# A two-layer diffusion backbone on one core: the order of seven products, the place of bank copies, and where the modulation is computed

## The chip, the cores and the metric

The kernel runs on one core of one Trainium2 chip. The metric is device time in microseconds (us). Before the change three runs gave 2406.03, 2399.41 and 2404.97 us, median 2404.97. PE is TensorE, PEld its weight loads, DVE is VectorE, ACT is ScalarE, POOL is GpSimd, SP is SyncE; a q behind a name (SPq, POOLq) is that engine's DMA queue.

## The reference, cut to what matters

Two streams of 256 tokens each, a latent one and a context one, go through two layers with the same weights. A layer is a half-step SwiGLU feed-forward, a token mixing (mLSTM and latent attention side by side), and a second half-step feed-forward. Each is preceded by a norm and modulated by nine rows that come from a conditioning vector:

```
mx = split(silu(c)     @ w_ada[l] + b_ada[l], 9)      # latent
mc = split(silu(c_ctx) @ w_ada[l] + b_ada[l], 9)      # context
x   = x   + 0.5*mx[2]*swiglu(rmsnorm(x,  g1)*(1+mx[1])+mx[0], w_ff1_up, w_ff1_dn)
ctx = ctx + 0.5*mc[2]*swiglu(rmsnorm(ctx,g1)*(1+mc[1])+mc[0], w_ff1_up, w_ff1_dn)
y_ctx, y_lat = token_mix(...)      # modulated by groups 3, 4; scaled by group 5
x   = x + mx[5]*y_lat
x   = x + 0.5*mx[8]*swiglu(rmsnorm(x, g3)*(1+mx[7])+mx[6], w_ff2_up, w_ff2_dn)
# the context stream does the same, but not behind the mixing of the last layer
```

The model width is 1024, the feed-forward width 2816. All is float32; the kernel computes each product as three matmuls of a high and a low part (hi*hi, lo*hi, hi*lo).

## The kernel before, in words

**Parts of a weight.** A weight block of 128x1024 is loaded into a buffer `st` (six of them), ACT copies it to a rounded high part `wh`, and DVE subtracts to get the low part `wl` (four buffers of each). This is `unit` for plain blocks and `Step.weights` with `parts7` for the blocks of the seven products.

**The seven products.** The second feed-forward of layer 0 and the first of layer 1 (`ff7`) go over both streams. Their up-projection treats the two halves of the width and the two streams as a 2x2 block product and uses seven products in place of eight. Four of the 22 blocks of the feed-forward width go the plain way (`FIRST`); the others are nine `Step`s of two blocks. A step needs four quarters of weights, a11, a12, a21, a22, and seven weights made from them: 1 is a11, 2 is a12, 4 is a22, 5 is a21+a22, 6 is 5+a11, 7 is a11+a21, 3 is 6+a12. Before the change DVE forms 5 (L715), and the other three sums are made by DMAs that POOL issues and that add into the buffer (`more`, L704). Each product is 24 matmuls. The results gather in three PSUM banks: 1, 6, 7 and 4 add up in A (rA), 2 and 3 in B (rB), 5 in C (rC). After 1, 6 and 7 ACT copies what bank A holds to a tile sa, sb or sc (L763) before the next of them adds to it. So product 6 cannot start until the copy behind 1 is done, 7 not until the copy behind 6, 4 not until the copy behind 7. The order of the products is a list in `ff7`, and each product's first matmul is held behind the last of the one before.

**Order on the engines.** The program is planned: an instruction has the place of its call, moved forward by `high_priority(offset)` (110 for the weights of a step, 150 for plain blocks, 40 for the bank copies), and a planner with a model of the times fixes one order for each engine, which each engine then works through in that order. `issue_after(x)` holds an instruction behind x on the same engine.

**Chunks.** The steps are done in chunks of one, four and four (`CHUNKS`). At the end of a chunk `last_blocks` multiplies what it gave by the down weights, eight blocks, and adds to the residual.

**Modulation.** Group g of layer l is computed by DVE: 8 blocks of 128 rows of w_ada, each loaded as two 128x512 pieces, and for each piece and stream one instruction that multiplies by the conditioning row and sums (L397). The class `Ada` holds a list of blocks; `drip` in the feed-forwards, and `Feed.pump` in the mixing, work it off as the stage goes on, and loads run two blocks ahead. On its first call it also loads and activates the conditioning rows (`silu_rows`: cb is the load, ACT and DVE make cs). Layer 0's second feed-forward computes groups 0 to 2 of layer 1; layer 1's first computes groups 3 to 6; the mLSTM part of layer 1's mixing computes groups 7 and 8. From group 5 on layer 1 needs the latent stream alone.

Of the kernel before, what the change touches and what calls it, by code (L numbers as in the profile page):

```python
# [50 lines left out]
SLOW = (3, 2)  # L51
EARLY = 2
SOON = 40
EVERY = 10
TAIL = 2
START = ((4, 4), (4, 4))
MARKS = (7, 7, 7, 7, 7, 7)
# [88 lines left out]
def body(ctx, tc, A):  # L146
# [183 lines left out]
        for s in range(2):  # L330
            mods[l, s] = cp.tile([P, 72], F32, name=f"mod{l}{s}")

    def silu_rows():

        res = {}
        for s in range(2):
            for q in range(2):
                v = act(F32, "cb")[:, :512]
                load(v, cc.partition_broadcast(P)[:, s, q * 512 : (q + 1) * 512])
                res[s, q] = act(F32, "cs")[:, :512]  # L340
                silu2(res[s, q], v)
        return res
# [39 lines left out]
    def ada_load(l, g, j):  # L382
# [4 lines left out]
            sts.append(st)  # L387
        return sts

    def ada_block(cb, l, g, j, sts):  # L390
        t = g * 8 + j
        streams = (0, 1) if l < DEPTH - 1 or g < 5 else (1,)
        for q, st in enumerate(sts):
            for s in streams:
                o = st if s == streams[-1] else act(F32, "junk")[:, :512]
                dst = mhalf[:, s, t : t + 1] if q else mods[l, s][:, t : t + 1]
                V.scalar_tensor_tensor(o, st, 0.5, cb[s, q], ALU.mult, ALU.mult, accum_out=dst)  # L397

    def ada_group_end(l, g):
        streams = (0, 1) if l < DEPTH - 1 or g < 5 else (1,)  # L400
        c = COLS["b_ada", l] + g * 8
        for s in streams:
            m = mods[l, s][:, g * 8 : g * 8 + 8]
            V.tensor_tensor(m, m, mhalf[:, s, g * 8 : g * 8 + 8], ALU.add)
            V.tensor_tensor(m, m, vecs[:, c : c + 8], ALU.add)
            if g % 3 == 1:
                gn = COLS[("g_n1", "g_n2", "g_n3")[g // 3], l]
                V.scalar_tensor_tensor(m, m, 1.0, vecs[:, gn : gn + 8], ALU.add, ALU.mult)
            elif g in (2, 8):
                V.tensor_scalar(m, m, 0.5, None, ALU.mult)  # L410

    class Ada:
# [8 lines left out]
            while len(self.loaded) < min(upto, self.n):  # L421
                self.loaded.append(ada_load(*self.todo[len(self.loaded)]))

        def next(self):
            if self.done < self.n:
                self.run((self.done + 1) / self.n)

        def run(self, frac):

            if self.cb is None:  # L430
                self.cb = silu_rows()
            while self.done < min(self.n, round(frac * self.n)):
                self.load(self.done + self.ahead)
                l, g, j = self.todo[self.done]
                ada_block(self.cb, l, g, j, self.loaded[self.done])
                if j == 7:
                    ada_group_end(l, g)
                self.done += 1
            self.load(self.done + self.ahead)
# [144 lines left out]
    def ff(l, f, streams, queue, after):  # L584
        g0 = 0 if f == 0 else 6
        cols = slice(0, T) if len(streams) == 2 else LAT
        n = T if len(streams) == 2 else HALF
        step = [0.0]

        def drip(w):  # L590
            step[0] += w
            if queue:
                queue.run(step[0] / (2 * CH + 0.7 * (2 * KB - 3)))

        def at(dst, part):
            return [d[:, part.start - cols.start : part.stop - cols.start] for d in dst]

        for c in range(2):
            blocks = range(c * CH, (c + 1) * CH)
            keys = {i: [("up", l, f, i, u) for u in range(2)] for i in blocks}  # L600
            gs = [pair(n) for _ in blocks]
            early = []
            if c == 0:
                for i in blocks[:2]:
                    early.append((i, units(keys[i], UW, 4)))
                    if ahead[0] > 1:
                        ahead[0] = EARLY
                for part in (LAT, CTX) if len(streams) == 2 else (LAT,):
                    for i, lhs in early:
                        up(part, hpairs(part), None, lhs, at(gs[i], part))  # L610
                drip(2.0)
            for i in blocks[len(early) :]:
                up(cols, hpairs(cols), keys[i], None, at(gs[i - c * CH], cols))
                drip(1.0)
                ahead[0] = AHEAD

            def make(nb, c=c):
                r = []
                for u, (a, b) in enumerate(DN_SPLIT):
                    r += units([("dn", l, f, c, nb, u)], (b - a) * P, b - a)  # L620
                drip(0.7)
                return r

            norms = {s: Norm((CTX, LAT)[s]) for s in streams} if c else None
            last_blocks(make, gs, streams, l, g0 + 2, norms, lambda s: after(norms[s], s))
        if queue:
            queue.run(1.0)

    hx = {}

    def shifted(nm, l, s, g):

# [51 lines left out]
    class Step:  # L686
# [18 lines left out]
            return self.st[n]  # L705

        def weights(self, r):
            with tc.high_priority(offset=AHEAD_S):
                if r == 1:
                    st = self.fresh("a", "a11")  # L710
                elif r == 2:
                    st = self.fresh("b", "a12")
                elif r == 5:
                    st = self.fresh("c", "a21")
                    V.tensor_tensor(st, st, self.fresh("d", "a22"), ALU.add)  # L715
                elif r == 6:
                    st = self.more("c", "a11")
                elif r == 7:
                    st = self.more("a", "a21")
                elif r == 3:  # L720
                    st = self.more("c", "a12")
                else:
                    st = self.st["d"]
                hi = wp.tile([P, UW], F32R, tag="wh", name="wh", bufs=WB)
                lo = wp.tile([P, UW], F32R, tag="wl", name="wl", bufs=WB)
                parts7(st, hi, lo)
            w = "p (b k n) -> p b k n"
            return hi.rearrange(w, b=2, k=4), lo.rearrange(w, b=2, k=4)

# [28 lines left out]
        def after(self, r):  # L758
            v, ps = self.v, self.ps
            if r in (1, 6, 7):  # L760
                with tc.high_priority(offset=SOON):
                    v[r] = self.tile("s" + "abc"[(1, 6, 7).index(r)])
                    S.activation(v[r], ps[1], AF.Copy)  # L763
            if r == 2:
                v[2] = self.tile("a7")
                with tc.high_priority(offset=SOON):
# [17 lines left out]
    def ff7(l, f, queue, after):  # L784
# [10 lines left out]
        for c, (first, n) in enumerate(CHUNKS):  # L795
            gs = []
            if first:
                keys = [[("up", l, f, i, u) for u in range(2)] for i in range(first)]
                early = [(i, units(keys[i], UW, 4)) for i in range(2)]
                for s, part in ((1, LAT), (0, CTX)):  # L800
                    for i, lhs in early:
                        if s:
                            gs.append({})
                        hi, lo = pair(HALF)
                        up(part, hpairs(part), None, lhs, (hi, lo))
                        gs[i][s] = hi, lo
                        if s == 0 and i == 1:
                            rest = differences()
                            next(rest)
# [6 lines left out]
            t0 += n  # L816
            for st in mine:
                t = st.t
                order = [(t, 1), (t, 2), (t, 6), (t + 1, 5), (t, 7), (t, 3), (t, 4)]
                if t == 0:  # L820
                    order.insert(0, (t, 5))
                if t == STEPS - 2:
                    order.insert(6, (t + 1, 1))
                if t == STEPS - 1:
                    order = [(t, 6), (t, 2), (t, 7), (t, 3), (t, 4)]
                for u, r in order:
                    mark = steps[u].product(r, mark)
                    drip(1 / 7)
                gs += [{s: st.dst[s][i] for s in (0, 1)} for i in range(2)]
# [9 lines left out]
            queue.run(1.0)  # L839


    def mix(l, queue, after):
        last = l == DEPTH - 1
        allc = slice(0, T)
        qc = LAT if last else allc
# [9 lines left out]
        class Feed:  # L855
# [3 lines left out]

            def __init__(self):  # L860
                self.items, self.chains, self.slow, self.done = [], [], [], set()
                self.pumps, self.queue = 0, None

            def add(self, key, gen):
                self.items.append((key, gen))
# [14 lines left out]
            def pump(self, n=1):  # L880
                self.draw(self.chains, n)
                for _ in range(n):
                    self.pumps += 1
                    if self.queue and self.pumps % EVERY == 0:
                        self.queue.next()
                    if self.pumps % SLOW[last] == 0:
                        self.draw(self.slow, 1)

# [660 lines left out]
        due = 0.0  # L1549
        for h, rate in chain(((-1, FEED[last][0]) for _ in mla()), ((h, FEED[last][1]) for h in mlstm())):  # L1550
            due += rate
            feed.queue = queue if h >= 0 else None
            feed.step(int(due), room_for(h))
            due -= int(due)

        if queue:
            queue.run(1.0)


        ys = []  # L1560
# [54 lines left out]

    for l in range(DEPTH):
        last = l == DEPTH - 1
        half(l, 0, Ada(0, range(2, 9), 2) if l == 0 else Ada(l, range(3, 7), 2), normed(l, None, 3))
        mix(l, Ada(l, range(7, 9), 2) if last else None, normed(l, 1, 6))
        half(l, 1, None if last else Ada(l + 1, range(3), 2), final if last else normed(l + 1, 0, 0))  # L1620

# [119 lines left out]
```

## Time and profile before

| | |
|---|---|
| median of 3 runs | 2404.97 us (2399.41 to 2406.03) |
| profiled execution, and its span | 2411.98 us, 2410.3 us |
| PE busy, DVE busy, ACT busy | 2313.2, 1746.2, 1093.2 us |
| granted TensorE clock, mean over the span | 0.982 |
| first seven-product stage (layer 0, second feed-forward) | 1026 to 1404 us |
| second seven-product stage (layer 1, first feed-forward) | 1404 to 1787 us |
| mixing of layer 1 | 1787 to 2207 us |
| last feed-forward (latent stream alone) | 2207 to the end |

How to read it: a wait is listed as who waited, for whom, the total, how often, and the longest. A row of the timeline has the start, the duration, engine, line, operation and tiles, and in brackets the idle time of that engine just before and what ended it. A clock of 1.00 is 2.4 GHz, 0.50 is 1.2 GHz.

### The profile page before, as it was taken

How to read it: one execution, taken by the hardware profiler on the slowest of the kernel's cores; microseconds unless marked ns; L12 is line 12 of the kernel's file. 1: busy time of each engine (PE TensorE's matmuls, PEld its weight loads, DVE VectorE, ACT ScalarE, POOL GpSimd, SP SyncE). 2: the span in 40 equal slices, each digit the busy share in tenths (PEclk: the TensorE clock that was granted, in tenths of full speed). 3: DMA queues.
4: the chain of work that ended last, by engine and by line, in shares of the span. 5: the costliest groups of instructions: out<-in, count | busy, mean ns of one | idle time of the engine just before them, and what ended most of it. 6: DMA issues, size and time to landing. Idle time of an engine off the chain costs nothing. (4 is left out here: it accounts for less than half of the span.)

```text
span 2410.3 us, 39446 instructions
## 1 busy us (share of the span) xinstructions
PE 2313.2 (96%) x15390; PEld 2101.8 (87%) x15390; DVE 1746.2 (72%) x3559; ACT 1093.2 (45%) x1778; POOL 147.2 (6%) x298
## 2 busy tenths in 40 slices
PE   7999999999999999999999999999899998999998
PEld 4888888888898888889999988999898797999998
DVE  6887787796577654487877678896768778876665
ACT  6322223567544442363534353443446564455443
POOL 1121110000100000000001000000000000000000
PEclk9999999999999999999999999999999999999999
DMA  9657545222222223446868526786722345455563
GB/s 331 196 158 229 158 143 164 77 63 62 68 76 76 71 79 96 124 104 186 216 175 195 148 79 201 186 245 166 200 80 82 89 130 168 140 168 156 171 207 105
DMA packets 117113, 347.66 MB, mean 144 GB/s; under 512 B 13886, under 2 KB 16190, under 8 KB 116926
## 3 DMA queue, kind: packets, MB, share of 16 engines
q1 hardware_dynamic: 100190, 287.47, 38.1%
q0 software_dynamic: 16736, 57.68, 10.8%
q8 instruction: 120, 1.97, 0.3%
q14 instruction: 67, 0.55, 0.1%
HBM read 341.95 MB, written 3.15 MB: 143 GB/s over the span
## 5 line engine op out<-in xcount | busy, mean ns | idle before, releaser
L246 ACT ACTIVATE wh<-st 128x1024 fp32r<-128x1024 f32 (+3 forms) x396 | 391.6, 992 | 674.2 <-issue 219.2
L248 DVE TENSOR_TENSOR wl<-st,wh 128x1024 fp32r<-128x1024 f32 (+3 forms) x396 | 450.0, 1140 | 221.5 <-ACT wh L246 220.0
L653 ACT ACTIVATE wh<-st 128x1024 fp32r<-128x1024 f32 x126 | 133.4, 1060 | 216.1 <-PE dn L511 63.1
L654 DVE TENSOR_TENSOR wl<-st,wh 128x1024 fp32r<-128x1024 f32 x126 | 153.6, 1221 | 39.4 <-ACT wh L653 39.2
L397 DVE SCALAR_TENSOR_TENSOR ada<-ada,cs 128x512 f32<-128x512 f32 x256 | 168.9, 688 | 17.1 <-DMA ada<-ada 17.0
L293 PE MATMUL p<-hl,wh 128*128 128x256 f32 (+1 forms) x536 | 180.1, 336 | 0.0
L292 PE MATMUL p<-hh,wh 128*128 128x512 f32 (+1 forms) x512 | 174.1, 340 | 0.0
L294 PE MATMUL p<-hh,wl 128*128 128x512 f32 (+1 forms) x512 | 173.3, 339 | 0.0
L505 DVE SCALAR_TENSOR_TENSOR x<-dn,mod,x 128x256 f32<-128x256 f32 x168 | 75.4, 479 | 98.7 <-PE dn L268 50.4
L397 DVE SCALAR_TENSOR_TENSOR junk<-ada,cs 128x512 f32<-128x512 f32 x192 | 124.4, 687 | 3.5 <-DMA ada<-ada 3.5
L741 PE MATMUL rA<-dh,wh 128*128 128x256 f32 x288 | 88.1, 306 | 37.0 <-ACT sa L763 35.6
L293 PE MATMUL pb<-hl,wh 128*128 128x512 f32 (+1 forms) x352 | 120.5, 342 | 0.0
L294 PE MATMUL pa<-hh,wl 128*128 128x512 f32 (+1 forms) x352 | 120.5, 342 | 0.0
L294 PE MATMUL pb<-hh,wl 128*128 128x512 f32 (+1 forms) x352 | 120.5, 342 | 0.0
L292 PE MATMUL pb<-hh,wh 128*128 128x512 f32 (+1 forms) x352 | 120.5, 342 | 0.0
L293 PE MATMUL pa<-hl,wh 128*128 128x512 f32 (+1 forms) x352 | 120.5, 342 | 0.0
L292 PE MATMUL pa<-hh,wh 128*128 128x512 f32 (+1 forms) x352 | 120.5, 342 | 0.0
L293 PEld LDWEIGHTS p<-hl,wh 128*128 128x128 f32 x536 | 101.4, 189 | 11.0
L294 PEld LDWEIGHTS p<-hh,wl 128*128 128x128 f32 x512 | 96.8, 189 | 11.3
L292 PEld LDWEIGHTS p<-hh,wh 128*128 128x128 f32 x512 | 96.9, 189 | 10.9
L268 PE MATMUL dn<-hi,wh 128*128 128x512 f32 (+1 forms) x278 | 101.1, 365 | 0.0
L268 PE MATMUL dn<-hi,wl 128*128 128x512 f32 (+1 forms) x278 | 101.1, 364 | 0.0
(438 smaller groups left out, 7190.4 us busy)
## 6 DMA issues: line engine op xcount, KB each, us to landing
st<-wall SPq DMA_DIRECT2D x372, 512.0 KB, 3.7
ada<-ada SPq DMA_DIRECT2D x176, 256.0 KB, 5.3
ada<-ada POOLq DMA_DIRECT2D x112, 256.0 KB, 3.5
st<-wall POOLq DMA_DIRECT2D x54, 512.0 KB, 5.7
st<-wall SPq DMA_DIRECT2D x56, 384.0 KB, 3.3
st<-wall SPq DMA_DIRECT2D x32, 320.0 KB, 3.0
cb<-cc SPq DMA_DIRECT2D x16, 256.0 KB, 4.4
x<-xT SPq DMA_DIRECT2D x8, 256.0 KB, 5.9
```

The source lines that it names most:

```text
L246: S.activation(hi[:, :n], st[:, :n], AF.Copy)
L248: V.tensor_tensor(lo[:, :n], st[:, :n], hi[:, :n].bitcast(F32), ALU.subtract)
L268: TE.matmul(ps, lhs[k][a][:, lsl], rhs[k][b][:, rsl], start=i == 0, stop=i == 3 * n - 1)
L292: TE.matmul(ps, a, b, start=first, stop=False)
L293: TE.matmul(ps, a, bl, start=False, stop=False)
L294: TE.matmul(ps, al, b, start=False, stop=final_)
L397: V.scalar_tensor_tensor(o, st, 0.5, cb[s, q], ALU.mult, ALU.mult, accum_out=dst)
L505: V.scalar_tensor_tensor(xs[nb][:, cols], ps[:, pcols], mod(l, s, g, nb), xs[nb][:, cols], ALU.mult, ALU.add)
L653: S.activation(hi, t, AF.Copy)
L654: V.tensor_tensor(lo, t, hi.bitcast(F32), ALU.subtract)
L741: mm = TE.matmul(ps[:, p * HALF : (p + 1) * HALF], w[x][:, p, k], hx["op", r][k][y], start=new and i == 0, stop=i + 1 == len(todo), skip_g ...
```

## The change

The list of products is reordered, so that 1 and 2 of the next step come in among the last of the present one. Bank copies are remembered in `snaps`, and the copy that makes a high part is held behind one of them (`BEFORE` says which). Weight 5 is now made by a load and an adding DMA, weight 3 by DVE from the buffers of 2 and 6. The conditioning rows are begun earlier in `ff7` (`begin`), for only the streams that are used. Group 7 moves to layer 1's first feed-forward, group 8 to its second, and the mixing computes none.

```
-EVERY = 10
+BEFORE = {5: 1, 7: 1, 3: 1, 1: 6, 4: 6, 2: 7, 6: 7}
...
-                queue.run(step[0] / (2 * CH + 0.7 * (2 * KB - 3)))
+                queue.run(min(1.0, step[0] / (CH - 1 if queue.n == KB else 2 * CH + 0.7 * (2 * KB - 3))))
...
-    hx = {}
+    hx, snaps = {}, {}
...
+        def begin(self):
+            l, g, _ = self.todo[0]
+            self.cb = silu_rows(streams_of(l, g))
...
                 elif r == 5:
-                    st = self.fresh("c", "a21")
-                    V.tensor_tensor(st, st, self.fresh("d", "a22"), ALU.add)
+                    self.fresh("c", "a21")
+                    st = self.more("c", "a22")
...
                 elif r == 3:
-                    st = self.more("c", "a12")
+                    st = self.st["b"]
+                    V.tensor_tensor(st, st, self.st["c"], ALU.add)
                 else:
-                    st = self.st["d"]
+                    st = self.fresh("d", "a22")
...
-                parts7(st, hi, lo)
+                snap = snaps.get(BEFORE[r])
+                with tc.issue_after(snap) if snap else nullcontext():
+                    S.activation(hi, st, AF.Copy)
+                V.tensor_tensor(lo, st, hi.bitcast(F32), ALU.subtract)
...
-                    S.activation(v[r], ps[1], AF.Copy)
+                    snaps[r] = S.activation(v[r], ps[1], AF.Copy).ins
...
                         gs[i][s] = hi, lo
+                        if s and i and queue:
+                            queue.begin()
...
-                order = [(t, 1), (t, 2), (t, 6), (t + 1, 5), (t, 7), (t, 3), (t, 4)]
+                order = [(t, 6), (t + 1, 5), (t, 7), (t, 3), (t + 1, 1), (t, 4), (t + 1, 2)]
                 if t == 0:
-                    order.insert(0, (t, 5))
-                if t == STEPS - 2:
-                    order.insert(6, (t + 1, 1))
+                    order = [(0, 5), (0, 1), (0, 2)] + order
                 if t == STEPS - 1:
                     order = [(t, 6), (t, 2), (t, 7), (t, 3), (t, 4)]
+                elif t == STEPS - 2:
+                    order.pop()
...
-        half(l, 0, Ada(0, range(2, 9), 2) if l == 0 else Ada(l, range(3, 7), 2), normed(l, None, 3))
-        mix(l, Ada(l, range(7, 9), 2) if last else None, normed(l, 1, 6))
-        half(l, 1, None if last else Ada(l + 1, range(3), 2), final if last else normed(l + 1, 0, 0))
+        half(l, 0, Ada(0, range(2, 9), 2) if l == 0 else Ada(l, range(3, 8), 2), normed(l, None, 3))
+        mix(l, normed(l, 1, 6))
+        half(l, 1, Ada(1, range(8, 9) if last else range(3), 2), final if last else normed(l + 1, 0, 0))
```

## Rows read from the trace of the kernel before

**Rows 1.** The page: the span, and busy time of each engine.
```profile
span 2410.3 us, 39446 instructions
...
PE 2313.2 (96%) x15390; PEld 2101.8 (87%) x15390; DVE 1746.2 (72%) x3559; ACT 1093.2 (45%) x1778; POOL 147.2 (6%) x298
```
**Rows 2.** Waits of PE, whole span: who, for whom, total us, times, longest.
```profile
PE rA L741 <- ACT sa L763: 35.6, 8, 7.2
PE s L268 <- ACT qh L941: 12.9, 2, 9.3
```
**Rows 3.** Timeline of PE at seven of those eight waits: start, us, instruction, idle before.
```profile
1088.97 0.58 PE L741 MATMUL rA<-dh,wh 128*128 128x256 f32 x1 [5.65 <-ACT sa L763]
...
1188.31 0.38 PE L741 MATMUL rA<-dh,wh 128*128 128x256 f32 x1 [3.83 <-ACT sa L763]
...
1212.19 0.38 PE L741 MATMUL rA<-dh,wh 128*128 128x256 f32 x1 [2.38 <-ACT sa L763]
...
1340.95 0.58 PE L741 MATMUL rA<-dh,wh 128*128 128x256 f32 x1 [4.83 <-ACT sa L763]
...
1469.41 0.58 PE L741 MATMUL rA<-dh,wh 128*128 128x256 f32 x1 [5.65 <-ACT sa L763]
...
1551.15 0.58 PE L741 MATMUL rA<-dh,wh 128*128 128x256 f32 x1 [5.18 <-ACT sa L763]
...
1724.89 0.58 PE L741 MATMUL rA<-dh,wh 128*128 128x256 f32 x1 [7.17 <-ACT sa L763]
```
**Rows 4.** Timeline of ACT just ahead of three of the late bank copies.
```profile
1087.80 0.63 ACT L319 ACTIVATE cs<-cb 128x512 f32<-128x512 f32 x1 [2.66 <-DMA cb<-cc]
...
1186.71 1.06 ACT L653 ACTIVATE wh<-st 128x1024 fp32r<-128x1024 f32 x1 [2.97 <-DMA st<-wall]
...
1722.78 0.63 ACT L653 ACTIVATE gh<-t 128x512 fp32r<-128x512 f32 x1 [6.50 <-DVE t L753]
```
**Rows 5.** Timeline of DVE ahead of the third of these.
```profile
1719.09 0.69 DVE L397 SCALAR_TENSOR_TENSOR ada<-ada,cs 128x512 f32<-128x512 f32 x1 [6.77 <-DMA ada<-ada]
```
**Rows 6.** Windows over the seven products behind the waits of rows 3: stretch, busy by engine.
```profile
sum 32.63, PE 32.62 PEld 32.63 DVE 23.84 ACT 4.26 POOL 0.00; mean PE 4.66 PEld 4.66 DVE 3.41 ACT 0.61 POOL 0.00
```
**Rows 7.** Windows: stretch, length, busy us of PE, PEld, DVE, ACT, POOL; clock, DMA.
```profile
1093.78:1096.61 2.83, 2.83 (x27) 2.83 (x26) 2.71 (x6) 1.55 (x2) 0.00 (x0) 1.00 0.04 13
1026.00:1404.00 378.00, 360.39 (x2868) 354.01 (x2869) 289.70 (x530) 164.79 (x238) 23.10 (x27) 0.97 0.62 165
1404.00:1787.00 383.00, 360.28 (x2865) 352.37 (x2864) 289.59 (x528) 164.45 (x237) 24.09 (x29) 0.97 0.64 175
1520.50:1608.20 87.70, 81.67 (x679) 81.11 (x678) 78.13 (x140) 42.95 (x55) 8.54 (x10) 0.98 0.83 214
...
2210.00:2290.00 80.00, 78.70 (x653) 78.70 (x654) 50.98 (x81) 39.60 (x60) 0.00 (x0) 0.96 0.51 153
```
**Rows 8.** Adding DMAs that POOL issues (L704), 1026 to 1787: durations, time to landing.
```profile
L704 POOL DMA_DIRECT2D st<-wall x54: 845/850/929, 1061.9 to 1712.0; - x54
...
DMA to landing us min/median/max: 5.2/5.7/8.8
```
**Rows 9.** Plain loads of quarters (L700), same stretch.
```profile
DMA to landing us min/median/max: 3.4/4.3/7.0
```
**Rows 10.** DVE's sum for weight 5 (L715), same stretch.
```profile
L715 DVE TENSOR_TENSOR st<-st x18: 1217/1226/1227, 1032.7 to 1691.1; 128x1024 f32<-128x1024 f32 x18
```
**Rows 11.** Waits of DVE in the four steps from 1520.5 to 1608.2 us.
```profile
DVE st L715 <- DMA st<-wall: 4.8, 3, 2.6
```
**Rows 12.** Windows in the mixing: DVE's modulation instructions (L397) alone, ahead of two waits.
```profile
2008.00:2036.20 28.20, 5.56 (x16) 0.92 0.57 186
2062.00:2083.00 21.00, 4.00 (x12) 1.00 0.50 154
```
**Rows 13.** Windows behind these two waits, all engines (columns as in rows 7).
```profile
2036.17:2042.10 5.93, 5.93 (x16) 4.87 (x17) 0.67 (x1) 0.00 (x0) 0.13 (x2) 0.50 0.22 85
...
2082.31:2086.50 4.19, 4.19 (x22) 4.19 (x23) 1.20 (x3) 0.00 (x0) 0.00 (x0) 0.59 0.74 246
```

More of the change, by code (lines that the diff above doesn't have):

```diff
@@ L331, in body, with silu_rows @@
             mods[l, s] = cp.tile([P, 72], F32, name=f"mod{l}{s}")
-    def silu_rows():
+    def silu_rows(streams):
         res = {}
-        for s in range(2):
+        for s in streams:
             for q in range(2):
@@ L388, in ada_load, with streams_of @@
         return sts
+    def streams_of(l, g):
+        return (0, 1) if l < DEPTH - 1 or g < 5 else (1,)
     def ada_block(cb, l, g, j, sts):
         t = g * 8 + j
-        streams = (0, 1) if l < DEPTH - 1 or g < 5 else (1,)
+        streams = streams_of(l, g)
         for q, st in enumerate(sts):
@@ L399, in ada_group_end @@
     def ada_group_end(l, g):
-        streams = (0, 1) if l < DEPTH - 1 or g < 5 else (1,)
+        streams = streams_of(l, g)
         c = COLS["b_ada", l] + g * 8
@@ L422, in load @@
                 self.loaded.append(ada_load(*self.todo[len(self.loaded)]))
-        def next(self):
-            if self.done < self.n:
-                self.run((self.done + 1) / self.n)
+        def begin(self):
+            l, g, _ = self.todo[0]
+            self.cb = silu_rows(streams_of(l, g))
         def run(self, frac):
             if self.cb is None:
-                self.cb = silu_rows()
+                self.begin()
             while self.done < min(self.n, round(frac * self.n)):
@@ L839, in ff7, with mix @@
             queue.run(1.0)
-    def mix(l, queue, after):
+    def mix(l, after):
         last = l == DEPTH - 1
@@ L861, in __init__ @@
                 self.items, self.chains, self.slow, self.done = [], [], [], set()
-                self.pumps, self.queue = 0, None
+                self.pumps = 0
             def add(self, key, gen):
@@ L883, in pump @@
                     self.pumps += 1
-                    if self.queue and self.pumps % EVERY == 0:
-                        self.queue.next()
                     if self.pumps % SLOW[last] == 0:
@@ L1551, in mix @@
             due += rate
-            feed.queue = queue if h >= 0 else None
             feed.step(int(due), room_for(h))
             due -= int(due)
-        if queue:
-            queue.run(1.0)
         ys = []
```

## The prediction, on record before the changed kernel ran

> **What bounds the kernel now.** I read four views in this order. The page first: PE is busy 2313.2 of 2410.3 us and DVE 1746.2 [rows 1], so a change that adds and removes no matmul can win only PE's idle time (97.1 us) and the time that PE spends at its lower clock. Then the waits of PE over the whole span: the largest is product 6 of a step (rA, L741) behind the bank copy sa, 35.6 us in eight waits, and the second the mLSTM scores behind qh, 12.9 us in two [rows 2]. Both lie in stages that the change touches. Then the timeline of PE for each wait's size [rows 3], and the timelines of ACT and DVE just ahead of it for what held the copy. A copy itself is short; each time it stood behind another ACT instruction that was waiting.
>
> There are three such causes [rows 4]. At the first step of each stage ACT waits for the load of the conditioning rows (cs behind cb): the two waits of 5.65 us. At 1186.71 ACT waits 2.97 us in the copy of a high part (wh) for a DMA. I followed that DMA back: it is the sum for weight 3, which POOL can issue only when weight 6 has been split. I put the waits of 3.83, 2.38, 4.83 and 5.18 us down to this. At 1722.78 ACT waits 6.50 us for DVE in the split of a step's output (gh), and DVE had itself waited 6.77 us for a piece of w_ada [rows 5]: the wait of 7.17 us. The eighth is 35.6 less the seven, 0.9 us.
>
> What comes behind such a wait is slow too. The seven products behind the seven waits take 32.63 us together [rows 6]; an unhindered one takes 2.83 [rows 7]. So 32.63 - 7 x 2.83 = 12.8 us is lost at the lower clock, 1.8 us for each wait on average. Waits and clock together: 35.6 + 12.8 = 48.4 us.
>
> The granted clock is 0.97 in both stages, 378 and 383 us long [rows 7]. The Trainium skill (TensorE: Matmul & The Clock Gate, Terms) prices the penalty as throttled time times the share of the clock that is lost, which here gives (378 + 383) x 0.03 = 22.8 us, and by that my sum below would be 10 us better. The products say 12.8, since part of the low-clock time falls on an idle PE and part on the start of a stage; I use the products.
>
> **The change part by part.**
>
> *Conditioning rows begun earlier.* `begin` stands behind the second latent block, four further block products and the differences ahead of where the first drip stood. This takes away both waits of 5.65 us and 2 x 1.8 of clock: 14.9 us. The activation can now hold ACT at the stage's start instead; its wait was 2.66 us there [rows 4], so for two stages between 0 and 5.3; I take 1. Net 13.9.
>
> *Weight 3 from DVE.* The DMA had from the split of 6 to the split of 3 three products, 3 x 2.83 = 8.5 us. It needs the split (1.06 on ACT [rows 4], 1.2 on DVE, as the sum of the same shape [rows 10]), 0.85 for the issue and 5.2 to 8.8 from issue to landing [rows 8]; 5.7 + 2.3 = 8.0 at the median and 11.1 at worst, so it comes late about half the time. Now DVE adds two buffers that are both there: 1.23 us in place of 5.7. DVE's load does not grow, since it no longer makes the sum for 5, of the same shape and count (18) [rows 10]. It also loses waits for DMA: 4.8 us in four steps alone [rows 11]. All four waits go: 3.83 + 2.38 + 4.83 + 5.18 = 16.2, and 4 x 1.8 of clock: 23.4 us.
>
> *Weight 5 by load and adding DMA.* Load 4.3 (3.4 to 7.0) [rows 9], add 5.7 (5.2 to 8.8) [rows 8], split 2.3: 12.3, at worst 18.1 us. Its buffer comes free when weight 3 of the step before has been added and split (1.2 + 2.3 = 3.5 us behind the end of product 2). From there to product 5 of the next step there are eight products in the new order (2 | 6, 5', 7, 3, 1', 4, 2', 6' | 5''), 22.6 us, so 19.1 are left. Even the worst fits, by 1.0. On POOL's queue this DMA now stands ahead of the one for 7, and on ACT its split stands ahead of the splits of 7 and 3 and the next copy: whoever is late makes these late. Price 0, bounds 0 and the slower rival below.
>
> *The order, and the edges of `BEFORE`.* Between 1 and 6 there are now two products (4, 2') instead of one, so the copy has 5.7 us of cover, not 2.8; between 7 and 4 there are also two (3, 1'); 7 keeps its one (5'), and in the last step 6 has one, as before. An edge holds the high part behind a copy of a product that is four back or more; with four wh buffers the part could not be written sooner anyway, so it costs ACT at most a copy's length, off the path (ACT is busy 164 of 383 us [rows 7]). The edges do not hold the output's split (gh) behind a copy. So of the wait of 7.17 us with its 1.8 and the 0.9 I count only 3.9 of 9.9: cover of 2.83 and about 1 of clock. Bounds 0 and 9.9.
>
> *DVE in the steps.* The four steps from 1520.5 hold 78.1 us of DVE work in 87.7 [rows 7]; without the wait of 5.18 and its clock they last about 81, so DVE would be 96% busy. What it waited for there was mostly the DMA that goes [rows 11], so it can fit, but the rest must spill into the down blocks. In the second stage there are 16 more modulation instructions of about 0.69 us (5.56 / 8, read-outs in) [rows 12]: 11 us over 383, with DVE idle for 93 [rows 7]. New waits of PE from this: between 0 and half of the gain; I take 5 us for both stages.
>
> *No modulation in the mixing.* DVE loses 32 such instructions. Ahead of the first wait for qh (9.3 of the 12.9 [rows 2]) there are 8, 5.56 us; ahead of the second (3.6) 6, 4.00 us [rows 12]. Of the first I found six in the stretch where DVE had no gap: 4.2 us. The second goes whole, 3.6. Clock: behind the second 4.19 us at 0.59, 1.7 lost; behind the first 5.93 at 0.50, 3.0 lost [rows 13], of which I take 1. Sum 10.5; as the planner lays this stretch out anew I take 9. Bounds 0 and 17.6 (12.9 + 4.7).
>
> *Group 8 in the last feed-forward.* 16 instructions, 11 us, beside 29 us of idle DVE in its first 80 us [rows 7]. It must end ahead of the first down block and has ten blocks for it. ACT can wait for cb once, 2.66 us [rows 4], behind four split parts; I take 1, bounds 0 and 7.4 (5.65 + 1.8).
>
> Sum: 13.9 + 23.4 + 3.9 - 5 + 9 - 1 = 44.2 us. Against the profiled time, 2411.98, that is 2368. The median of the runs lies 7.0 below the profiled one, so 2404.97 - 44 = **2361 us**.
>
> **The rivals.**
>
> *DVE becomes the bound.* At 96% over four steps every late wl goes straight to PE, and the waits come back under another name. Half of the two stages' 41.2 us is given back: 44.2 - 20.6 + 5 = 28.6 (the 5 is in it), 2376 us. For: the 78.1 of 81. Against: in the waits of PE there is none of a product for wl (the two largest are both behind ACT) [rows 2].
>
> *Weight 5 comes too late: slower.* Were its buffer taken by another load first, two products later (5.7 us), the chain at worst, 18.1, would miss the 19.1 by 4.7 in each of 16 steps (eight in a stage): 75 us, and 2361 + 75 = 2436. It decides from a mean miss of 44.2 / 16 = 2.8 us, that is a chain of 21.9 against rows that sum to 12.3 and 18.1. For: one more adding DMA hangs on a load, with DMA share 0.83 [rows 7]. Against: the lead of eight products.
>
> The Trainium skill (SBUF — State Buffer, SBUF: two separate sides) speaks for this rival: while DVE has the port that it shares with GpSimd, POOL cannot write the descriptors of its DMAs. The rows do not show it: 54 issues took 845 to 929 ns [rows 8] while DVE was busy 290 of 378 and of 383 us [rows 7]. By the rule each of 18 new issues could stand behind one DVE instruction, an estimate of 18 x 1.23 = 22 us, if they were on the path.
>
> *The copies stay late.* The edges hold only weight parts; if outputs' splits and activations stand ahead of the copies instead, only the conditioning rows (13.9) and the mixing (9) are won, and waits behind those splits take back as much as half of the stages' gain, 20: 2402, no change.
>
> *All of it goes*, mixing included: 48.4 + 17.6 = 66, 2339 us.
>
> **How the numbers follow.** Forecast (2347 to 2370) 0.60, DVE bound (2370 to 2390) 0.20, all gone 0.07, copies stay late 0.06, weight 5 late 0.07. What three or five runs can tell from no change is about 0.3%, 7.2 us. Faster 0.60 + 0.20 + 0.07 = 0.87, same 0.06, slower 0.07. The range leaves out the last two and the ends of the others: 2341 to 2387.
>
> **What would show it.** Right: no wait of L741 for sa over 1 us at the stage's first step; no ACT wait of wh for a DMA ahead of a sa copy; L715 gone and a DVE sum of the same length in its place; PE's wait for qh at 9.3 down to about 5, the other gone; granted clock of both stages 0.99. Wrong: L741 waiting for wh or wl of weight 5 or 3, DVE over 95% in the steps with PE idle beside it, new waits for cb in the last feed-forward, or a span within 7 us of 2410.

## The result, and the profile after

Four runs of the changed kernel took 2376.28 to 2379.71 us, median 2377.62; four of the kernel before beside them had a median of 2405.5. The ratio is 0.9885, 95% interval [0.9859, 0.9911]: faster by 28 us, where 44 were forecast. The direction is right and the time lies in the range, but it is the very time of the rival "DVE becomes the bound", 2376. Whether that rival was the cause is what most of the experiments are about.

The profiled execution took 2376.57 us; its clock is 0.989. Counted from the first matmul of a stage to the first of the next, in one profiled execution of each kernel:

| stage, us | before | after | gained | forecast |
|---|---|---|---|---|
| ahead of the first seven-product stage | 1026.3 | 1024.4 | 1.9 | 0 |
| first seven-product stage | 377.2 | 354.4 | 22.8 | 36.2 for both |
| second seven-product stage | 383.1 | 383.6 | -0.5 | |
| mixing of layer 1 | 424.6 | 413.4 | 11.2 | 9 |
| last feed-forward | 199.0 | 199.0 | -0.1 | -1 |
| span | 2410.3 | 2374.8 | 35.5 | 44.2 |

The spans differ by more than the medians do (35.5 against 28), since the profiled execution of before is one of its slower ones. The forecast gives one number, 36.2, for both seven-product stages; put down to the stages where its waits lay, its terms come to some 23 us in the first and 18 in the second, before the 5 that it took off for DVE. Against that the table is plain all the same: the first stage and the mixing gave about what was forecast, the second stage gave nothing.

The page after; PE is still busy for 97%, and DVE's sum has not changed [rows 1].
```profile
span 2374.8 us, 39424 instructions
...
PE 2302.4 (97%) x15390; PEld 2091.6 (88%) x15390; DVE 1744.7 (73%) x3557; ACT 1088.6 (46%) x1776; POOL 143.7 (6%) x298
```
The waits of PE after, whole span (who, for whom, total us, times, longest).
```profile
PE rA L750 <- ACT sa L772: 13.6, 6, 5.7
...
PE rA L750 <- ACT sb L772: 5.9, 3, 2.4
...
PE s L268 <- ACT qh L950: 3.8, 2, 2.2
...
PE rB L750 <- DVE rB L779: 2.8, 2, 2.6
```
Against [rows 2], the 35.6 us behind the copy sa fell to 13.6 and the 12.9 behind qh to 3.8. But products behind the copy sb wait for 5.9 now (1.3 before) and products behind DVE's sum into rB for 2.8, which the forecast did not have. The windows after (columns as in [rows 7]) show in which stage: both stages whole, the four steps in the middle of each, and last one product.
```profile
1024.00:1378.80 354.80, 351.33 (x2865) 345.36 (x2866) 288.57 (x529) 163.41 (x237) 23.14 (x27) 1.00 0.65 176
1378.80:1762.40 383.60, 361.59 (x2866) 353.14 (x2865) 299.79 (x563) 163.14 (x237) 24.09 (x29) 0.98 0.67 186
1135.70:1214.40 78.70, 78.70 (x672) 78.69 (x672) 72.91 (x119) 41.74 (x53) 8.57 (x10) 1.00 0.86 224
1495.50:1589.80 94.30, 84.13 (x674) 83.36 (x674) 80.54 (x148) 41.16 (x53) 8.54 (x10) 0.95 0.76 201
...
1567.16:1572.65 5.49, 5.49 (x25) 5.49 (x26) 4.75 (x9) 3.31 (x4) 0.85 (x1) 0.50 0.62 166
```
Read the third and the fourth row together, the four middle steps of each stage. In the first stage DVE works for 72.91 of 78.70 us, 93%, and PE does not stop once. In the second DVE works for 80.54 of 94.30, only 85%, and PE is idle for 10.2. DVE's work alone would make these steps 80.54 us long at least, 1.8 more than the 78.70 of the first stage; the other 13.8 of the 94.30 are not for want of DVE's time. DVE idles, and PE with it.

The waits of DVE in the second stage show for what:
```profile
DVE ada L400 <- DMA ada<-ada: 25.0, 12, 4.5
```
The first stage has no such wait, and the second stage of the kernel before had 16.7 us of it in seven waits. The pieces do not take longer from issue to landing than in the first stage (pieces of w_ada, second stage, then first):
```profile
DMA to landing us min/median/max: 2.7/5.1/6.8
DMA to landing us min/median/max: 3.4/5.3/7.2
```
What is shorter is the lead. With the pieces matched in order in the trace, the median time from a piece's issue to the instruction that uses it last is 28.2 us in the first stage and 8.7 in the second.

The largest gap of PE in the second stage, and what led to it, in the timeline of each engine (start, us, engine, line, operation, tiles, idle time before and what ended it). DVE:
```profile
1551.18 0.69 DVE L400 SCALAR_TENSOR_TENSOR ada<-ada,cs 128x512 f32<-128x512 f32 x1 [3.17 <-DMA ada<-ada]
...
1551.80 2.35 DVE L735 TENSOR_TENSOR wl<-st,wh 128x1024 fp32r<-128x1024 f32 x2
...
1561.05 0.69 DVE L400 SCALAR_TENSOR_TENSOR ada<-ada,cs 128x512 f32<-128x512 f32 x1 [4.55 <-DMA ada<-ada]
...
1564.55 0.68 DVE L324 SCALAR_TENSOR_TENSOR t<-t,rB 128x512 f32<-128x512 f32 x1
1565.27 0.69 DVE L762 SCALAR_TENSOR_TENSOR t<-t,b 128x512 f32<-128x512 f32 x1
```
SP's queue:
```profile
1554.18 0.33 SPq L703 DMA_DIRECT2D st<-wall  x1
1554.56 1.24 SPq L386 DMA_DIRECT2D ada<-ada  x2
1564.66 0.33 SPq L703 DMA_DIRECT2D st<-wall  x1
```
ACT:
```profile
1554.05 0.58 ACT L319 ACTIVATE t<-rB 128x512 f32<-128x512 f32 x1
1565.99 0.63 ACT L656 ACTIVATE gh<-t 128x512 fp32r<-128x512 f32 x1 [11.37 <-DVE t L762]
1566.53 0.58 ACT L772 ACTIVATE sa<-rA 128x512 f32<-128x512 f32 x1
1567.01 1.99 ACT L734 ACTIVATE wh<-st 128x1024 fp32r<-128x1024 f32 x2
```
PE:
```profile
1567.16 0.58 PE L750 MATMUL rA<-dh,wh 128*128 128x256 f32 x1 [5.65 <-ACT sa L772]
```
Read in order of time, this is a ring. DVE waits 3.17 us for a piece of w_ada, and the low part wl behind it is late. The buffer of that weight comes free late, so SP's load st (L703), which waits for it, is issued late, at 1554.18: the wait, in SP's own waits, is `SPq L703 <- DVE wl L735`, 7.9 us. Behind that load on SP's queue stands the issue of the next piece of w_ada (1554.56). It lands some 6 us on, and DVE waits for it again, 4.55 us. Then the activation (L324, L762) is late, ACT is idle for 11.37 us ahead of the split of the step's output (gh), the copy sa stands behind gh, the weight parts that the change holds behind a copy stand behind sa, and PE waits 5.65 us. The product behind it takes 5.49 us at a clock of 0.50; those of before were slow too, 4.66 us on average [rows 6]. The first half of the ring shows at each of the twelve waits of the stage: on SP's queue every one of the twelve pieces stands behind a load of a weight that had itself waited for DVE, for 1.3 to 7.9 us, with at most two other pieces in between.

The waits of ACT in this stage give the sum of that (in the first stage the same wait is 22.8 us in eleven, the longest 4.9, and holds up no product in the middle steps):
```profile
ACT gh L656 <- DVE t L762: 38.7, 7, 11.4
```

### The profile page after: what moved, and what is told of

It reads as the page before. It is cut to its first block, busy times and chain, and to the rows that moved or that the text cites. A ratio compares the mean times of both kernels' runs of the same rounds, so it can differ in the third digit from the quotient of the medians.

```text
span 2374.8 us, 39424 instructions
## 1 busy us (share of the span) xinstructions
PE 2302.4 (97%) x15390; PEld 2091.6 (88%) x15390; DVE 1744.7 (73%) x3557; ACT 1088.6 (46%) x1776; POOL 143.7 (6%) x298
## 3 DMA queue, kind: packets, MB, share of 16 engines
q0 software_dynamic: 16736, 57.68, 10.9%
## 4 chain that ended last, share of the span: by engine, by line
PE 87%; DVE 7%; DMA 2%; ACT 2%; issue 2%; SPq 0%; DVEq 0%; ACTq 0%
PE dn L268 12%; PE dn L514 9%; PE rA L750 6%; PE p L292 4%; PE p L293 4%; PE p L294 4%; PE rB L750 3%; PE pb L293 3%; PE pa L293 3%; PE pa L294 3%; PE pa L292 3%; PE pb L292 3%; PE pb L294 3%; PE pv L268 2%; DMA ada<-ada 2%; PE pa L268 2%
## 5 line engine op out<-in xcount | busy, mean ns | idle before, releaser
L735 DVE TENSOR_TENSOR wl<-st,wh 128x1024 fp32r<-128x1024 f32 x126 | 152.9, 1222 | 19.6 <-ACT wh L734 19.2
L293 PEld LDWEIGHTS p<-hl,wh 128*128 128x128 f32 x536 | 100.7, 188 | 10.9
L292 PEld LDWEIGHTS p<-hh,wh 128*128 128x128 f32 x512 | 96.1, 188 | 10.9
L750 PE MATMUL rA<-dh,wh 128*128 128x256 f32 x288 | 84.2, 292 | 19.5 <-ACT sa L772 13.6
```

The source lines that it names most:

```text
L292: TE.matmul(ps, a, b, start=first, stop=False)
L293: TE.matmul(ps, a, bl, start=False, stop=False)
L735: V.tensor_tensor(lo, st, hi.bitcast(F32), ALU.subtract)
L750: mm = TE.matmul(ps[:, p * HALF : (p + 1) * HALF], w[x][:, p, k], hx["op", r][k][y], start=new and i == 0, stop=i + 1 == len(todo), skip_g ...
```

## The experiments

Each kernel is the changed one with one edit. All times in us; "second" is the second seven-product stage, "rest" the mixing and the last feed-forward; the ratio is against the kernel before on the same chip. The four stage columns come from one profiled execution of each kernel. The first stage of the seven kernels in which it is the same (the change and edits 1, 2, 5, 7, 11 and 12) took 354.0 to 356.8 us, and a profiled execution lay up to 6.2 us from the median of its kernel (edit 10). So differences of under some 3 us in a column say nothing, and in kernels whose runs scatter more, somewhat larger ones may not either.

| edit | ahead | first | second | rest | median | ratio, 95% |
|---|---|---|---|---|---|---|
| the change itself | 1024.4 | 354.4 | 383.6 | 612.4 | 2377.62 | 0.9885 [0.9859, 0.9911] |
| 1 loads four blocks ahead | 1025.6 | 356.1 | 378.8 | 612.3 | 2373.53 | 0.9875 [0.9855, 0.9894] |
| 2 no modulation in the second | 1023.6 | 356.8 | 355.0 | 612.2 | 2349.10 | 0.9776 [0.9751, 0.98] |
| 3 output's split behind the copy | 1026.1 | 354.3 | 372.2 | 610.2 | 2364.72 | 0.9836 [0.9817, 0.9856] |
| 4 old order, no edges | 1023.5 | 367.9 | 375.6 | 611.2 | 2381.33 | 0.9912 [0.989, 0.9934] |
| 5 group 7 left out | 1024.5 | 354.6 | 369.4 | 611.7 | 2362.46 | 0.9825 [0.9794, 0.9856] |
| 6 no edges | 1024.3 | 360.9 | 372.7 | 611.0 | 2374.72 | 0.9874 [0.9851, 0.9897] |
| 7 groups 5 to 8 early | 1034.7 | 356.0 | 355.7 | 610.6 | 2357.86 | 0.9806 [0.9785, 0.9826] |
| 8 edits 7 and 3 | 1035.9 | 353.9 | 357.1 | 609.5 | 2355.40 | 0.9792 [0.9766, 0.9817] |
| 9 old sums | 1024.3 | 361.7 | 382.7 | 609.2 | 2380.79 | 0.9904 [0.9889, 0.9919] |
| 10 conditioning rows late | 1023.5 | 359.3 | 382.0 | 610.4 | 2383.08 | 0.9917 [0.99, 0.9933] |
| 11 groups 5 to 7 early | 1029.7 | 354.0 | 357.6 | 611.5 | 2358.58 | 0.9806 [0.9792, 0.9821] |
| 12 groups 6 and 7 early | 1024.9 | 354.2 | 361.4 | 611.2 | 2354.40 | 0.9793 [0.9778, 0.9807] |

The first three ask what holds the second stage: the loads of w_ada (theory 1), DVE's work (rival 2), or ACT's order alone (rival 3).

**1. Loads of w_ada four blocks ahead.**
```diff
-... else Ada(l, range(3, 8), 2), ...
+... else Ada(l, range(3, 8), 4), ...
```


> The changed kernel, with the loads of w_ada in layer 1's first feed-forward (stage B) four blocks ahead instead of two. Theory 1 (pieces of w_ada come late: DVE waits 25.0 us for them in stage B, and splits of outputs that wait for DVE hold the bank copies): that wait falls under 8 us, stage B falls from 383.6 to 373 or less, in all about 2366. Rival 2 (there is simply too much DVE work in the steps): the wait for loads falls, but stage B stays above 379, in all 2373 to 2378.


Between the two: 378.8, at the edge of what rival 2 gave, and the median, 2373.53, lies in its range. But the wait, which both let fall, is mostly still there:
```profile
DVE ada L400 <- DMA ada<-ada: 17.3, 9, 3.1
```
An earlier place in the order does not bring a piece earlier where SP's queue is stopped by a load ahead of it. The lead from issue to last use is 9.7 us at the median, against 8.7. So this edit alone does not part the loads from the work: it takes away only a third of the wait.

**2. No modulation in the second stage.**
```diff
+    V.memset(mods[1, 1][:, 24:64], 0.5)
+    V.memset(mods[1, 0][:, 24:40], 0.5)
...
-... else Ada(l, range(3, 8), 2), ...
+... else None, ...
```


> The changed kernel without any modulation in stage B (groups 3 to 7 of layer 1 are left out and set to 0.5). Theory 1 and rival 2: the bank copies are in time as in the first such stage (354.4 us), stage B takes 353 to 360, in all about 2350. Rival 3 (ACT's order alone, outputs' splits and activations ahead of the copies whatever DVE waits for): stage B stays above 370, since the splits still stand there.


The second stage falls to 355.0, and there its window reads (columns as above):
```profile
1380.40:1735.40 355.00, 352.65 (x2867) 346.19 (x2866) 232.60 (x318) 162.36 (x233) 24.11 (x29) 1.00 0.54 139
```
PE is idle for 2.35 us and the clock is full. The new order and the sums can thus hold in this stage as in the first (the conditioning rows are gone with the modulation); the whole 28.6 us between 383.6 and 355.0 hang on the modulation, its work and its loads. ACT's order alone (rival 3) is out.

**3. The split of a step's output behind the next copy.**
```diff
-            parts7(t, hi, lo)
+            later.append(lambda: parts7(t, hi, lo))
...
+                    if r in (1, 6) or (t == STEPS - 1 and r == 4):
+                        while later:
+                            later.pop(0)()
```


> The changed kernel with the split of a step's outputs (gh, gl) issued behind the next bank copy (behind the copy of product 1 or 6) instead of ahead of it. Rival 3: the waits of PE for sa and sb (13.6 and 5.9 us) fall under 5 in all, stage B to about 362, in all 2357. Theory 1 and rival 2: the copies come earlier, but the weight parts on DVE are as late, so PE waits for wl instead; stage B stays above 375, in all above 2369.


In between again: 372.2, 11.4 less. ACT's waits in the second stage and DVE's:
```profile
ACT gh L656 <- DVE t L762: 11.7, 6, 2.6
```
```profile
DVE ada L400 <- DMA ada<-ada: 17.4, 9, 3.9
```
A late activation now holds the split but not the copy, and the ring turns more slowly. PE's waits move to the weights (4.1 us for wl). So ACT's order passes DVE's lateness on and makes it worse, and does not cause it.

**4. The old order of the products, without edges.**
```diff
-                with tc.issue_after(snap) if snap else nullcontext():
+                with nullcontext():
...
-                order = [(t, 6), (t + 1, 5), (t, 7), (t, 3), (t + 1, 1), (t, 4), (t + 1, 2)]
+                order = [(t, 1), (t, 2), (t, 6), (t + 1, 5), (t, 7), (t, 3), (t, 4)]
...
```


> The changed kernel with the products in the order of before and no high part held behind a copy; the sums, the early conditioning rows and the moved groups stay. If the late sum for weight 3 was the cause of the four waits, as predicted, the first stage stays within 6 us of 354.4 (before 377.2), in all 2378 to 2390. If the order and the held parts carry the gain, the first stage is above 365, in all above 2395.


The first stage answers for the order, though the whole stays under the 2395 that was expected with it. There the wait for the copy is back, while ACT waits only 2.3 us in all for a DMA to make a high part (15.8 before):
```profile
PE rA L750 <- ACT sa L772: 10.6, 5, 2.7
```
The stage takes 367.9. Of its 22.8 us the sums and the early rows made 9.3, and the order with the edges 13.5. In the second stage the old order is better by 8.0, which no theory had.

**5. Group 7 left out of the second stage.**
```diff
+    V.memset(mods[1, 1][:, 56:64], 0.5)
...
-... else Ada(l, range(3, 8), 2), ...
+... else Ada(l, range(3, 7), 2), ...
```


> The changed kernel with group 7 of layer 1 left out (set to 0.5), so that stage B (layer 1's first feed-forward) has the 32 blocks of modulation that it had before. If the moved group is what took stage B's gain: stage B falls from 383.6 to 365 or less. If the new order suffers from the modulation that was there already: stage B stays between 374 and 382, like the old order with 40 blocks (375.6).


369.4 lies between the two expectations. The moved group alone costs 383.6 - 369.4 = 14.2 us of time, for 16 instructions of 0.69 us, 11 us of DVE. And against the kernel before, with the same 32 blocks in this stage, the rest of the change gains 383.1 - 369.4 = 13.7 us, where the forecast's terms come to 18, or 13 if its 5 for DVE are taken off here. So the second stage did gain; the moved group took it back. This kernel also sets the two stages side by side (windows of the first and of the second, columns as above):
```profile
1024.50:1379.10 354.60, 351.50 (x2864) 346.28 (x2865) 288.41 (x528) 163.29 (x236) 23.11 (x27) 1.00 0.64 176
1379.10:1748.50 369.40, 357.64 (x2867) 348.98 (x2866) 289.11 (x528) 162.53 (x237) 24.05 (x29) 0.99 0.65 181
```
DVE has the same 528 instructions and the same work in both, 288.41 and 289.11, since groups 5 and 6 need one stream only. What differs is how many pieces of w_ada come in: 24 blocks, 48 pieces, in the first stage; 32 blocks, 64 pieces, in the second, with half the work on each of the later ones. And there DVE waits:
```profile
DVE ada L400 <- DMA ada<-ada: 14.8, 7, 3.5
```
So for the same work of DVE the second stage is 14.8 us longer. That speaks for the loads and against the work, though the stages differ in other things too.

**6. The new order without the edges.**
```diff
-                with tc.issue_after(snap) if snap else nullcontext():
+                with nullcontext():
```


> The changed kernel, its order of products and all else kept, but no high part held behind a bank copy. If the order gives the first stage its gain over the old order (354.4 against 367.9), it stays below 358 there. If the held parts do: 362 to 370. For stage B each theory expects the same step on top of 383.6: 0, or 8 to 15 more.


The edges are worth 6.5 us in the first stage and cost 10.9 in the second, a miss in sign there. (The profiled execution is 4.2 us below the median of this kernel, which lies only 2.9 below the change's, so the 10.9 may be some 3 too large.) In the second stage:
```profile
PE rA L750 <- ACT sa L772: 9.3, 3, 3.8
PE rA L750 <- ACT sb L772: 3.2, 2, 2.0
```
```profile
ACT gh L656 <- DVE t L762: 8.2, 9, 2.7
```
The wait of gh for DVE falls from 38.7 to 8.2, and DVE's own wait for pieces of w_ada from 25.0 to 10.8. Without edges ACT makes high parts while it would stand behind gh, so DVE's low parts and the buffers behind them come sooner. The edge that keeps a copy punctual also ties weight parts to whatever the copy stands behind.

**7. Groups 5 to 8 of layer 1 computed in layer 0's first feed-forward**, so that the second stage has 16 blocks.
```diff
-... Ada(0, range(2, 9), 2) if l == 0 else Ada(l, range(3, 8), 2), ...
+... Ada(0, [*range(2, 9), *range(5 + NMOD, 9 + NMOD)], 2) if l == 0 else Ada(l, range(3, 5), 2), ...
...
-... Ada(1, range(8, 9) if last else range(3), 2), ...
+... None if last else Ada(1, range(3), 2), ...
```


> The changed kernel with groups 5 to 8 of layer 1 computed in layer 0's first feed-forward, so that stage B keeps 16 blocks (groups 3 and 4) and the last feed-forward none. Theory (what DVE has to do and to load in stage B delays the splits that stand ahead of the copies): stage B 356 to 364, the first feed-forward not more than 3 us longer, in all 2352 to 2358. Rival: DVE's modulation there delays the first feed-forward by as much as stage B wins, in all above 2370.


The second stage takes 355.7 with all its remaining modulation in it, 27.9 less:
```profile
1390.70:1746.40 355.70, 352.96 (x2866) 346.38 (x2866) 271.66 (x460) 164.19 (x237) 24.09 (x29) 1.00 0.61 165
```
DVE has no wait for w_ada there. Sixteen blocks cost nothing, as in the first stage its 24. But the first feed-forward grew by 10.3 us (4.0 of it a wait for wl, 1.9 for wh), more than expected.

**8. Edits 7 and 3 together.**


> The same, with the splits of a step's outputs issued behind the next bank copy as well. If both causes add up: stage B 354 to 358, in all 2348 to 2354. If the splits hurt only while DVE is late: no more than 2 us below the run without this edit.


The order of the output's split matters only while DVE is late: 11.4 us in the second stage with 40 blocks, nothing that shows with 16 (357.1 against 355.7; the medians, 2355.40 and 2357.86, overlap in their runs).

**9. The old sums** (5 by DVE, 3 by an adding DMA) in the new order.
```diff
-                    self.fresh("c", "a21")
-                    st = self.more("c", "a22")
+                    st = self.fresh("c", "a21")
+                    V.tensor_tensor(st, st, self.fresh("d", "a22"), ALU.add)
...
-                    st = self.st["b"]
-                    V.tensor_tensor(st, st, self.st["c"], ALU.add)
+                    st = self.more("c", "a12")
```


> The changed kernel, new order and held parts kept, with the sums of before: weight 5 by DVE, weight 3 by the adding DMA. If the late DMA for weight 3 was worth what the prediction gave it (23.4 us over two stages, about 12 in the first), the first stage goes from 354.4 to 362 to 368. If the order alone gives the DMA time enough, it stays below 357.


The sum by VectorE is worth 7.3 us in the first stage: 361.7, just short of the 362 to 368 that the prediction's price asked for. In the second no gain shows: with the old sums the stage is 0.9 shorter.

**10. The conditioning rows begun at the first drip again.**
```diff
-                        if s and i and queue:
-                            queue.begin()
```


> The changed kernel with the conditioning rows begun at the first drip again. If the prediction's price holds (5.65 us and 1.8 of clock a stage, less the 1.6 that is left of the wait now), the first stage takes 358 to 361 instead of 354.4. If two products of cover hide the wait: below 356.


Early rows are worth 4.9 us in the first stage. In the second no gain shows: with late rows the stage is 1.6 shorter, but this profiled execution is 6.2 us below its kernel's median.

**11 and 12. A cheaper place for the moved groups**: in layer 0's first feed-forward, with their loads on POOL's queue; first groups 5 to 7, then 6 and 7 (24 blocks stay in the second stage). The diff is that of edit 12.
```diff
-            (nc.sync if l else nc.gpsimd).dma_start(st, ...)
+            (nc.sync if l and g not in (6, 7,) else nc.gpsimd).dma_start(st, ...)
...
+... Ada(0, [*range(2, 9), 6 + NMOD, 7 + NMOD], 2) if l == 0 else Ada(l, range(3, 6), 2), ...
```


> The changed kernel with groups 5, 6 and 7 of layer 1 in layer 0's first feed-forward, loaded through POOL's queue as that stage's other pieces are; group 8 stays in the last feed-forward. Stage B keeps 16 blocks: 355 to 357. If the 10.3 us that the first feed-forward grew with 32 blocks were due to loads through SP's queue, it grows by under 4 us now, in all 2348 to 2352. If they go with the number of blocks: 7 to 8 us, in all 2354 to 2358.

> The same with groups 6 and 7 only; stage B keeps 24 blocks (groups 3 to 5). If stage B's loss goes steadily with its blocks (28.5 us from 0 to 40, 14.2 from 32 to 40), it takes 357 to 362; the first feed-forward grows by 2 to 5 us; in all 2351 to 2358.


Three groups lengthen the first feed-forward by 5.3 us, between the two expectations, and two by 0.5, less than expected. With two the second stage keeps 24 blocks and some of the wait:
```profile
1379.10:1740.50 361.40, 354.60 (x2866) 347.74 (x2866) 280.52 (x494) 163.11 (x237) 24.08 (x29) 0.99 0.64 174
```
```profile
DVE ada L400 <- DMA ada<-ada: 6.8, 3, 2.8
```
Edit 12 has the lowest median of the kernels that compute the whole: 2354.40 us (2353.19 to 2355.92), 23 below the changed kernel and about 50 below the one before. Edit 8 (2352.66 to 2358.06) can't be told from it.

## Why the prediction was right in part, and the step that failed

**What held.** The mixing: 11.2 against 9; the qh waits are 2.22 and 1.60 us where about 5 and 0 stood in the forecast. The last feed-forward: -0.1 against -1; without group 8 there (edit 7) it takes 199.1 us, no less than the 199.0 with it. The first wait of each stage fell from 5.65 to 1.56 us, not under 1. The granted clock is 1.00 in the first stage and 0.98 in the second, where 0.99 stood for both. Weight 5 was never late: PE waits 0.3 us in all for a low part of rC, the product of weight 5, and for no high part of the seven products, so the slower rival is out. POOL's 54 issues of adding DMAs took 842 to 1199 ns, median 855, against 845 to 929 before [rows 8]: the longest is 0.3 us longer, and PE waited for none of these DMAs. So the lock of the shared port that the Trainium skill (SBUF — State Buffer, SBUF: two separate sides) speaks of does not show here. For the writing of descriptors the section ties it to VectorE operations in a mode with two ports, and no run shows whether any here runs in one.

**What was right in sum, wrong in its parts.** In the first stage 22.8 us came, about the 23 of its terms, and in part by luck. I had put down the waits behind late copies to the DMA for weight 3 and the order to little: 23.4 and 3.9 over both stages. Undone one at a time in that stage, the sums are worth 7.3, the rows 4.9, the edges 6.5; the order and the edges together 13.5. (Undone singly such parts need not add up: where one is missing another covers for it.) The waits of 3.83, 2.38 and 4.83 were thus only in part the DMA's; in good part the copy stood too close to the product that needs it. So the term for weight 3 was too large and the term for the order too small.

**The step that failed: "DVE in the steps".** "11 us over 383, with DVE idle for 93", and "between 0 and half of the gain; I take 5 us for both stages". Nothing of it shows in the first stage; in the second it cost all of the gain: 14.2 us for the moved group alone (edit 5), 28.6 for all the modulation there (edit 2). Two things were overlooked. The 93 us of idle DVE is an average of the stage: the blocks fall into the steps, and in the trace of before DVE already waited 6.77 us there for a piece of w_ada [rows 5], 16.7 us in seven waits over the stage. And I treated that wait as one accident, though it was the first sight of the ring: the loads stand on SP's queue behind loads of weights which wait for DVE. A third thing was put at nothing: the edges, "at most a copy's length, off the path". In the first stage that held, but in the second they cost 10.9 us (edit 6): in the trace the weight parts held behind the copy sa start at 1567.01, behind the late split ahead of that copy (1565.99).

Time in the second stage against its blocks, all with the change's order: 0 blocks 355.0, 16 blocks 355.7 and 357.6, 24 blocks 361.4, 32 blocks 369.4, 40 blocks 383.6. Nothing up to 16, then 4 to 6, 8 and 14 us for each further group. DVE's waits for pieces go with it: none with 0 and 16 blocks, then 6.8, 14.8 and 25.0 us, where the stage is 6.4, 14.4 and 28.6 longer than with none. And so does the lead from issue to last use: 39.6 us with 16 blocks (edit 7), 14.8 with 24, 12.0 with 32, 8.7 with 40. My reading: so long as the pieces are punctual they are free, and each that is late makes later ones late. That it is the pieces, and not the instructions that I had counted, is borne out by this and by the two stages of edit 5, which have the same DVE work and differ by 14.8 us (they differ in other things too, as in what follows them); no edit of the loads alone shows it.

**The rival of the same time.** "DVE becomes the bound" said that half of both stages' gain comes back. Its number was right by chance: none came back in the first stage and all in the second. Its mechanism, DVE at 96% and wl late, did not show: in the four middle steps DVE ran at 93% in the first stage without a gap and at 85% in the second with gaps, and in the second stage PE waited 16.7 us for copies, 2.8 for DVE's sum into rB and 0.3 for wl. "The copies stay late" named the link on ACT that was there (a copy behind an output's split) but not its cause.

**What stays open.** The ring is read from the trace and not broken by itself: loads of w_ada on a queue of their own in the second stage were not tried, and edit 1 took away only 7.7 of the 25.0 us of wait. So how much of the 28.6 us is the loads' alone isn't known to the microsecond; nor why 24 blocks leave 6.8 us of wait in the second stage (edit 12) and none in the first, with a lead of 14.8 us there and 28.2 here. Also why the first feed-forward bears two more groups for 0.5 us, three for 5.3 and four for 10.3: the number of groups and the queue of their loads changed together.

## What to carry to other kernels

Count slack by stretch and by what is punctual, not by a stage's average: here an engine at 93% held nothing up, and at 85% it did, where what it waited for was issued behind something that waited for it. When work is moved to a stage, follow its loads along their queue to what releases the loads ahead of them; if that is the same engine, look for a ring, and try the work in another stage instead (two groups cost 0.5 us in the first feed-forward here). An edge that fixes the order on an engine gained 6.5 us here where its releaser was on time and cost 10.9 where it was not, so measure it in each stage.

## What the runs showed of the hardware

The clock can fall behind a gap and not in it, and a gap of the same length need not be followed by a fall. In the second stage after the change, PE stood still for 2.23 us ahead of 1537.47; the first matmuls behind the gap ran at full clock, and then it halved, in the midst of a product with PE busy. Ahead of 1547.22 PE stood still for 2.29 us, and behind that the clock stayed full (windows, columns as above):
```profile
1537.47:1538.75 1.28, 1.28 (x10) 1.28 (x11) 1.28 (x4) 1.28 (x2) 0.00 (x0) 1.00 0.92 320
1538.89:1541.50 2.61, 2.61 (x15) 2.61 (x14) 2.61 (x7) 1.89 (x3) 0.58 (x1) 0.50 0.28 105
1547.22:1552.00 4.78, 4.78 (x40) 4.78 (x41) 1.61 (x5) 3.39 (x4) 0.85 (x1) 1.00 0.88 260
```
Of the stage's four gaps from 2.2 to 2.6 us, two were followed by a fall (those of 2.23 and 2.39 us) and two were not (2.29 and 2.58). Over the whole stage the gaps are paid for more than once: PE was idle for 383.60 - 361.59 = 22.0 us, and busy for 361.59 where 351.33 do in the first, 10.3 us more.
